# Parameter rows on another DMA queue, a weight quarter moved between transposes, and a last step ordered by token halves

## The chip, the cores and the metric

The kernel runs on one core of a Trainium2 chip. A core has five engines that run their own instruction streams and meet at semaphores: TensorE (PE in the profile; PEld is its weight load), VectorE (DVE), ScalarE (ACT), GpSimd (POOL) and SyncE (SP). Transfers run on 16 DMA engines; SyncE, ScalarE and GpSimd can each issue them through a queue of their own. The metric is the time of one execution on the device in microseconds: lower is better. Runs of the kernel before took 3287.82 to 3290.53 us, median 3289.65 us.

## The reference

One layer of a hybrid backbone over 640 tokens of width 2048: 512 latent tokens and 128 context tokens, all in float32. Cut to what the change touches:

```
sh1, sc1, g1, sh2, sc2, g2 = split(silu(c) @ w_mod + b_mod, 6)   # c for latents, c_ctx for context
h = rmsnorm(x, norm1_g) * (1 + sc1) + sh1
p = h @ w_in
...                                    # RWKV-7 time mixing and a gated MLP over p, then x + g1 * (.. @ w_out)
h = rmsnorm(x, norm2_g) * (1 + sc2) + sh2
ff = (silu(h @ w_ffn_gate) * (h @ w_ffn_up)) @ w_ffn_down
x = x + g2 * ff
y = rmsnorm(x, final_norm_g)           # the two big outputs, 512 x 2048 and 128 x 2048
```

The start computes `sc1` and `sh1` (shift and scale) and the first `h`; the end computes `... @ w_ffn_down`, the last residual sum and the final norm. The "parameter rows" are `mu_shift`, `w0`, `a0`, `k_k`, `k_a`, `r_k`, `gn_w`, `gn_b` and `norm2_g`, small vectors that the middle of the layer needs with one channel per partition.

## The kernel before

The program is written in a tile language. A planner sets each engine's order from data dependences and program order; it may move an instruction ahead of others that are not ready yet. Within the start block TensorE's order is kept as written by hand. A pool of n buffers lets n tiles of one tag be in flight; a transfer into a tile waits until the n-th tile before it has been read.

**Start (lines 212 to 348).** Tokens lie as five tiles of 128 rows. SyncE loads them (`xall`, 1 MB each), then the weights `w_mod`, in pieces `wt` of 1 MB with five buffers, and pieces of `w_in`. For each token tile the loop at line 235 squares it (ScalarE), forms `1/sqrt` on GpSimd (`rsqrt`, line 135), scales it (VectorE), and transposes it in 16 blocks on TensorE into `xnT` (line 246), copied out by VectorE and ScalarE in turn.

`quarter(g, j)` (line 297) computes 512 of the 2048 columns of scale (g = 1) or shift (g = 0): four steps, each one `wt` load and its products (line 308), a copy `ms`, four transposes and the sum into `mc`. It is a generator, and the caller decides what runs between its steps. The loop at line 333 goes over j = 0..3: `quarter(1, j)`, then `quarter(0, j)`, with products of the quarter before (`products`, three column blocks of `w_in`, lines 165 and 188) between the steps; then `h_hi` and `h_lo` for four blocks of channels. After j = 1 `rows()` issues twenty small loads on SyncE's queue (lines 265 to 278) into `rowA` and `rowB`, and after j = 2 `params()` transposes the two tiles on TensorE and copies them into `prm`.

**Middle.** Nothing in it is changed.

**End (lines 1815 to 1977).** The product with `w_ffn_down` is done for six chunks of its rows and eight pairs of column blocks n, 48 steps. Each step is one round of `seven` (line 1588): seven block products in place of eight (Strassen's scheme, in Winograd's form), in the order `PORD` = 1, 2, 3, 7, 5, 6, 4. GpSimd forms the four differences of weight blocks (`combine`); two of them, for products 6 and 4, are made in the middle of the step in the place of their sources. Every weight block is split into a rounded part `hi` (ScalarE, line 1396) and a rest `lo` (VectorE, line 1397), and a product is twelve matmuls of 320 columns, half of the tokens. In the last chunk each product's PSUM bank is first filled with the sum so far (`filled`, lines 1917 and 1918).

What follows a product is a hook, run some products later in program order (`lag`, 3 at the end). For the last chunk the hooks are those of `Last` (line 1850): they combine the seven results of step n into `cs`, two column blocks by 640 tokens, multiply by `g2` and add `x` (`out`, line 1856), and then transpose the blocks back into token rows, copy them into `acc` and add up their squares in `sse` (`rows`, line 1891). Work put into `later` runs once the next step has reached a given product: `out` for the second half of tokens after o = 2, `rows` after o = 4 (`ROWO`). For the last step, n = 0, both run after its seventh product.

When all is done, `sse` is summed over the blocks, `1/sqrt` comes from GpSimd for all five token tiles at once, and ten output tiles of 128 x 1024 (line 1968) are formed: six in one instruction on VectorE (line 1976), four by ScalarE (line 1973) and then GpSimd (line 1974). SyncE stores each.

Of the kernel before, what the change touches and what calls it, by code (L numbers as in the profile page):

```python
# [10 lines left out]
F32 = mybir.dt.float32  # L11
# [8 lines left out]
P = 128  # L20
# [37 lines left out]
FRONT = 4  # L58
REST = 6
# [28 lines left out]
def flow_step(ctx: ExitStack, tc, x_prompt, x_sample, state_rwkv, c, c_ctx, w_mod, b_mod,  # L88
# [115 lines left out]
    with ExitStack() as ph:  # L204
# [29 lines left out]
        xnT = p0.tile([P, KB, T], F32, name="xnT")  # L234
        for t in range(NT):
            xt = xall[:, t, :]
            ss = p0b.tile([P, 1], F32, name="ss")
            S.activation(junk, xt, AF.Square, accum_out=ss)
            V.tensor_scalar(ss, ss, 1.0 / D, RMS_EPS, op0=ALU.mult, op1=ALU.add)
            rs = p0b.tile([P, 1], F32, name="rs")  # L240
            rsqrt(rs, ss)
            V.tensor_scalar_mul(xt, xt, rs[:, 0:1])
            for q in range(4):
                pt = ps0.tile([P, 4, P], F32, tag="pt", name="ptx")
                for b in range(4):
                    TE.transpose(pt[:, b, :], xt[:, (4 * q + b) * P:(4 * q + b + 1) * P], ident)
                (S.copy if q % 2 else V.tensor_copy)(xnT[:, 4 * q:4 * q + 4, t * P:(t + 1) * P], pt)

# [7 lines left out]

        rowA = p0.tile([P, P], F32, name="rowA")
        rowB = p0.tile([P, P], F32, name="rowB")
        G.memset(rowB, 0.0)
        G.memset(rowA, 0.0)  # L260
        nA = C_W0

        def rows():
            for m in range(4):
                nc.sync.dma_start(rowA[C_MU + 24 * m:C_MU + 24 * m + 24, :],
                                  mu_shift[0, m, 0:3072].rearrange("(r p) -> r p", p=P))
                nc.sync.dma_start(rowA[C_MU2 + 2 * m:C_MU2 + 2 * m + 2, :],
                                  mu_shift[0, m, 3072:3328].rearrange("(r p) -> r p", p=P))
                nc.sync.dma_start(rowA[C_MU3 + m:C_MU3 + m + 1, 0:32], mu_shift[0, m:m + 1, 3328:3360])
            for off, src in ((C_W0, w0[0].rearrange("d (r p) -> (d r) p", p=P)),  # L270
                             (C_A0, a0[0].rearrange("d (r p) -> (d r) p", p=P)),
                             (C_KK, k_k[0].rearrange("(r p) -> r p", p=P)),
                             (C_KA, k_a[0].rearrange("(r p) -> r p", p=P)),
                             (C_RK, r_k[0].rearrange("(r h) n -> r (h n)", h=2)),
                             (C_GW, gn_w[0].rearrange("(r h) n -> r (h n)", h=2)),
                             (C_GB, gn_b[0].rearrange("(r h) n -> r (h n)", h=2)),
                             (C_N2, norm2_g[0].rearrange("(r p) -> r p", p=P))):
                nc.sync.dma_start(rowB[off - nA:off - nA + src.shape[0], :], src)

        def params():  # L280
            pp = ptE.tile([P, 4, P], F32, tag="ptE", name="pp")
            TE.transpose(pp[:, 0, :], rowA, ident)
            TE.transpose(pp[:, 1, :], rowB, ident)
            V.tensor_copy(prm[:, 0:nA], pp[:, 0, 0:nA])
            V.tensor_copy(prm[:, nA:C_N1], pp[:, 1, 0:C_N1 - nA])
            V.tensor_copy(prm[:, C_N2:NPRM], pp[:, 1, C_N2 - nA:NPRM - nA])

        psx.close()
        h_hi = hpool.tile([P, KB, T], F32R, tag="h_hi", name="h_hi")
        h_lo = hpool.tile([P, KB, T], F32R, tag="h_lo", name="h_lo")  # L290
        pe = pex.enter_context(tc.tile_pool(name="pe", bufs=6, space=PSUM))
        early = [[pe.tile([P, HALF], F32, tag="big", name="big") for _ in range(2)] for _ in FIRST]
# [30 lines left out]

        def products(j):
# [1012 lines left out]
    PORD = (1, 2, 3, 7, 5, 6, 4)  # L1337

# [249 lines left out]
    def seven(b11, b12, b21, b22, x, hook, nk=4, bank=fresh, last=True):  # L1588
# [6 lines left out]
        src = {1: b11, 2: b21, 3: b22, 7: t3, 5: b12, 6: b22, 4: b21}  # L1595
        order = [raw for i in PORD for raw in src[i]]

        ready = [parts(order.pop(0), nk)]
        for o, i in enumerate(PORD):
# [12 lines left out]
            if i == 3:  # L1612
# [204 lines left out]
    sse = dn.tile([P, NT, 8], F32, name="sse")  # L1817
# [32 lines left out]
    class Last:  # L1850
# [11 lines left out]
        def __call__(self, o, p):  # L1862
# [20 lines left out]
            elif o == 6:  # L1883
# [3 lines left out]
                later.append((2, lambda: (self.out(1, 1), self.out(0, 1))))  # L1887
                later.append((ROWO, self.rows))
# [15 lines left out]

    later = []
    NC = len(CHK)

    fill = [(n, i) for n in range(7, -1, -1) for i in PORD]
# [13 lines left out]
    for s, (c, n) in enumerate(steps):  # L1922
# [15 lines left out]
        for o in seven(b11, b12, b21, b22, lambda i, k: XD[i, k], None if turn else Last(n) if final else Sum(n),  # L1938
                       CHK[c], bank, not turn):
# [13 lines left out]
            if s == len(steps) - 1 and o == 5:  # L1953
                while hooks:
                    hooks.pop(0)()
# [7 lines left out]
    rs = dn.tile([P, NT], F32, name="rse")  # L1963
    V.tensor_reduce(out=rs, in_=sse, axis=AX.X, op=ALU.add)
    V.tensor_scalar(rs, rs, 1.0 / D, RMS_EPS, op0=ALU.mult, op1=ALU.add)
    rsqrt(rs, rs)
    fg = acc[:, :, 5 * HALF:5 * HALF + 256]
    for t in range(NT):
        for h in range(2):
            out = fin.tile([P, 4, 256], F32, tag=f"out{h}", name="out")  # L1970
            src, f = (ap[:, 4 * h:4 * h + 4] for ap in (acc[:, :, t * 256:(t + 1) * 256], fg))
            if t == 1 or t == 3:
                S.activation(out, src, AF.Copy, scale=rs[:, t:t + 1])
                G.tensor_tensor(out=out, in0=out, in1=f, op=ALU.mult)
            else:
                V.scalar_tensor_tensor(out=out, in0=src, scalar=rs[:, t:t + 1], in1=f, op0=ALU.mult, op1=ALU.mult)
# [31 lines left out]
```

## Time and profile before

| | |
|---|---|
| median of 3 runs | 3289.65 us (3287.82 to 3290.53) |
| the profiled execution | 3287.43 us, its span 3285.6 us |
| mean granted clock of TensorE | 0.985 |
| TensorE busy | 3141.3 us (96%) |
| VectorE busy | 2401.2 us (73%) |
| ScalarE busy | 1458.3 us (44%) |
| GpSimd busy | 1260.1 us (38%) |

The profile covers one execution. A row of a stage view (two times, then five busy times) is a stretch of the span with the busy time of each engine, the granted clock, the share of the 16 DMA engines and what they moved. A row of the timeline is start, duration, engine, line of code, instruction, output<-inputs, and in brackets how long the engine was idle before it and what ended that. A row of waits is engine and line, what it waited for, the total, the count and the longest. A queue ("SPq") holds the issues of transfers, not the transfers themselves. Matmuls are pipelined, so a busy TensorE is not one at its peak.

### The profile page before, as it was taken

The numbers are of one execution on the slowest core, as the hardware profiler recorded it, in microseconds if no ns is written. First come the engines' busy times: TensorE is split into PE (matmuls) and PEld (weight loads), VectorE is DVE, ScalarE is ACT, GpSimd is POOL, SyncE is SP. The second block draws the span as 40 slices with busy tenths as digits, with TensorE's granted clock in tenths as the row PEclk, the third lists the DMA queues.
The fourth block names the chain that finished last, engine by engine and source line by source line (L and its number), as shares of the span: only waits on it lengthen the run. The fifth ranks groups of instructions, "written<-read, shape, count | busy, mean of one in ns | idle before, by whom it ended". The sixth has DMA issues, their size and how long they took to land.

```text
span 3285.6 us, 72386 instructions
## 1 busy us (share of the span) xinstructions
PE 3141.3 (96%) x28216; PEld 2905.3 (88%) x28216; DVE 2401.2 (73%) x4152; ACT 1458.3 (44%) x3179; POOL 1260.1 (38%) x1098
## 2 busy tenths in 40 slices
PE   6899999999999999999999999999999999999996
PEld 3688888778887887889899999999999999999996
DVE  4447766776866677767877787777787777877787
ACT  3334444444444444346644444444444444444365
POOL 0001122221222113332166566566565555555543
PEclk9899999999999999999999999999999999999998
DMA  8767776767668588756434433433433454553453
GB/s 318 244 185 219 188 204 188 181 184 206 178 185 222 137 272 277 240 152 182 127 114 120 123 116 116 127 116 116 127 116 116 127 183 149 158 164 122 132 160 119
DMA packets 740142, 550.88 MB, mean 168 GB/s; under 512 B 140712, under 2 KB 673208, under 8 KB 730968
## 3 DMA queue, kind: packets, MB, share of 16 engines
q1 hardware_dynamic: 727480, 532.57, 54.3%
q0 software_dynamic: 9984, 13.13, 1.7%
q8 instruction: 222, 3.64, 0.5%
q14 instruction: 120, 0.98, 0.1%
q10 hardware_dynamic: 2336, 0.57, 0.1%
HBM read 437.79 MB, written 110.95 MB: 167 GB/s over the span
## 4 chain that ended last, share of the span: by engine, by line
PE 75%; DVE 9%; issue 6%; DMA 5%; POOL 3%; ACT 2%; SPq 0%; DVEq 0%; ACTq 0%; POOLq 0%
PE P L1611 15%; PE P L1609 15%; PE P L1610 15%; PE big L188 4%; PE big L190 4%; PE big L189 4%; PE pG L636 2%; PE pm L881 2%; DMA raw<-in_w_in_dram 2%; PE big L1455 1%; PE big L1456 1%; PE big L1457 1%; DMA wt<-in_w_mod_dram 1%; PE pblk L820 1%; DVE mx L781 1%
## 5 line engine op out<-in xcount | busy, mean ns | idle before, releaser
L1611 PE MATMUL P<-xo,lo 128*128 128x320 f32 x2352 | 728.1, 310 | 2.5 <-DVE lo L1397 2.5
L1609 PE MATMUL P<-xo,hi 128*128 128x320 f32 x2352 | 727.4, 309 | 0.7 <-ACT hi L1396 0.7
L1610 PE MATMUL P<-xo,hi 128*128 128x320 f32 x2352 | 727.4, 309 | 0.0
L1397 DVE TENSOR_TENSOR lo<-raw,hi 128x512 fp32r<-128x512 f32 x526 | 507.3, 967 | 171.4 <-ACT hi L1396 167.3
L1396 ACT CAST hi<-raw 128x512 fp32r<-128x512 f32 x526 | 327.2, 622 | 489.6 <-PE P L1610 388.7
L188 PE MATMUL big<-h_hi,hi 128*128 128x320 f32 x1376 | 450.8, 328 | 8.5 <-ACT hi L166 5.0
L1611 PEld LDWEIGHTS P<-xo,lo 128*128 128x128 f32 x2352 | 442.1, 188 | 3.8 <-DVE lo L1397 3.8
L1609 PEld LDWEIGHTS P<-xo,hi 128*128 128x128 f32 x2352 | 442.0, 188 | 1.0 <-ACT hi L1396 1.0
L1610 PEld LDWEIGHTS P<-xo,hi 128*128 128x128 f32 x2352 | 441.9, 188 | 0.0
L190 PE MATMUL big<-h_hi,lo 128*128 128x320 f32 x1376 | 435.1, 317 | 1.3 <-DVE lo L167 1.3
L189 PE MATMUL big<-h_lo,hi 128*128 128x320 f32 x1376 | 434.0, 315 | 0.7 <-DVE h_lo L345 0.7
L1525 POOL TENSOR_TENSOR raw<-raw 128x512 f32<-128x512 f32 x252 | 407.4, 1626 | 15.3 <-DVE lo L1397 3.9
L1611 PE MATMUL P<-xd,lo 128*128 128x320 f32 x1232 | 383.7, 311 | 13.8 <-DVE lo L1397 13.5
L1609 PE MATMUL P<-xd,hi 128*128 128x320 f32 x1232 | 381.8, 310 | 3.5 <-ACT hi L1396 1.7
L1610 PE MATMUL P<-xd,hi 128*128 128x320 f32 x1232 | 380.6, 309 | 0.0
L167 DVE TENSOR_TENSOR lo<-raw,hi 128x512 fp32r<-128x512 f32 x268 | 185.1, 693 | 204.7 <-ACT hi L166 198.3
L188 PEld LDWEIGHTS big<-h_hi,hi 128*128 128x128 f32 x1376 | 262.8, 191 | 74.0 <-issue 46.6
L166 ACT CAST hi<-raw 128x512 fp32r<-128x512 f32 x268 | 165.1, 618 | 250.8 <-PE big L189 124.8
L1396 ACT CAST hi<-rawd 128x512 fp32r<-128x512 f32 (+1 forms) x288 | 168.8, 587 | 242.1 <-PE P L1610 193.4
L190 PEld LDWEIGHTS big<-h_hi,lo 128*128 128x128 f32 x1376 | 263.2, 191 | 7.4 <-DVE lo L167 3.2
L189 PEld LDWEIGHTS big<-h_lo,hi 128*128 128x128 f32 x1376 | 263.3, 191 | 6.9 <-issue 3.5
L1611 PEld LDWEIGHTS P<-xd,lo 128*128 128x128 f32 x1232 | 231.2, 188 | 20.6 <-DVE lo L1397 20.2
(380 smaller groups left out, 6257.8 us busy)
## 6 DMA issues: line engine op xcount, KB each, us to landing
wt<-in_w_mod_dram SPq DMA_DIRECT2D x96, 1024.0 KB
raw<-in_w_ffn_gate_dram SPq DMA_DIRECT2D x182, 256.0 KB
raw<-in_w_ffn_up_dram SPq DMA_DIRECT2D x182, 256.0 KB
rec<-d_S SPq DMA_DIRECT2D x80, 576.0 KB
raw<-in_w_in_dram SPq DMA_DIRECT2D x172, 256.0 KB
rawd<-in_w_ffn_down_dram SPq DMA_DIRECT2D x128, 256.0 KB
raw<-in_w_out_dram SPq DMA_DIRECT2D x96, 256.0 KB
xd<-d_os SPq DMA_DIRECT2D x66, 320.0 KB
```

Of the source, the lines that this page charges most:

```text
L166: S.copy(hi, raw)
L167: V.tensor_sub(lo, raw, hi.bitcast(F32))
L188: TE.matmul(halves[hf], hi[:, k, :], h_hi[:, kb, s], start=(kb == 0), stop=False)
L189: TE.matmul(halves[hf], hi[:, k, :], h_lo[:, kb, s], start=False, stop=False)
L190: TE.matmul(halves[hf], lo[:, k, :], h_hi[:, kb, s], start=False, stop=(kb == KB - 1))
L636: TE.matmul(two[h][:, cc - c0, :], XZ[:, cc, h, :, :].rearrange("p s t -> p (s t)"), R[:, cc, :, :].rearrange("p s t -> p (s t)"), start=T ...
L1396: S.copy(hi[:, 0:nk], raw[:, 0:nk])
L1397: V.tensor_sub(lo[:, 0:nk], raw[:, 0:nk], hi[:, 0:nk].bitcast(F32))
L1525: G.tensor_tensor(out=o[:, 0:nk], in0=p[:, 0:nk], in1=q[:, 0:nk], op=ALU.subtract)
L1609: TE.matmul(ps, hi[:, k, :], xk[:, 0, :], start=f, stop=False)
L1610: TE.matmul(ps, hi[:, k, :], xk[:, 1, :], start=False, stop=False)
L1611: TE.matmul(ps, lo[:, k, :], xk[:, 0, :], start=False, stop=l)
```

## The change

At the start:

- The transposes of `rowC` (`pp`, `bmod`) and the memsets of `rowA` and `rowB` stand ahead of x's loop.
- `lead = quarter(1, 0)` is made before x's loop, and one of its steps runs after each of token tiles 2, 3 and 4 (`BEGIN` = 2). The loop over j goes on with what is left of it.
- `rows()` is called right after x's loop and issues its twenty loads on GpSimd's queue; `params()` is called after j = 1.

At the end, for the last step (n = 0) alone:

- The products are taken in the order `PEND` = 1, 6, 7, 5, 4, 3, 2. Products 6 and 4 have buffers of their own for their differences, made at the start of the step. Hooks run without lag.
- The class `End` adds each product to `cs` as it comes (`put`), in an order that completes the second half of the tokens after the fifth product, one column block of the first half after the sixth and the other after the seventh. Token tiles 3 and 4 are turned, squared and scaled (`scale`) after the fifth, tiles 0, 1 and 2 in two parts after the sixth and seventh.
- The step before it (n = 1) has its `out` and `rows` called after products 0 and 1 of the last step, not 2 and 4.

The outputs come in the order of token tiles 3, 4, 0, 1, 2. VectorE forms nine of the ten; ScalarE forms one (tile 3, second half), for which `acc` has been multiplied by `final_norm_g` in the last step (`EARLY`). GpSimd forms none.

```diff
-            for i, _ in enumerate(itertools.chain(quarter(1, j), quarter(0, j))):
+            for i, _ in enumerate(itertools.chain(lead if j == 0 else quarter(1, j), quarter(0, j))):
...
+        lead = quarter(1, 0)
         for t in range(NT):
...
                 (S.copy if q % 2 else V.tensor_copy)(xnT[:, 4 * q:4 * q + 4, t * P:(t + 1) * P], pt)
+            if t >= BEGIN:
+                next(lead)
+        rows()
...
-                nc.sync.dma_start(rowB[off - nA:off - nA + src.shape[0], :], src)
+                nc.gpsimd.dma_start(rowB[off - nA:off - nA + src.shape[0], :], src)
...
             if j == 1:
-                rows()
-            if j == 2:
                 params()
...
+    PEND = (1, 6, 7, 5, 4, 3, 2)
...
+        s6, s4 = b22, b21
+        if end:
+            s6, s4 = ([xap.tile([P, 4, P], F32, tag=next(wtags), name="rawd")] for _ in range(2))
+            combine(s6, b22, b12)
+            combine(s4, b21, s6)
...
-                later.append((2, lambda: (self.out(1, 1), self.out(0, 1))))
-                later.append((ROWO, self.rows))
+                later.append((2 if n > 1 else 0, lambda: (self.out(1, 1), self.out(0, 1))))
+                later.append((ROWO if n > 1 else 1, self.rows))
...
+    class End(Last):
+        def put(self, m, h, src, base):
+            for (lo, hi, v) in seg(h):
+                s = slice(h * HALF + lo, h * HALF + hi)
+                V.scalar_tensor_tensor(out=self.cs[m][:, s], in0=src[:, lo:hi], scalar=modc[5][:, 2 * self.n + m, v:v + 1],
+                                       in1=base[m][:, s], op0=ALU.mult, op1=ALU.add)
...
+            elif o == 4:
+                self.put(0, 1, p, cs)
+                pr = pP.tile([P, 2, 256], F32, tag="P", name="prd")
+                self.turn(pr, 0, 3, (1, 0))
+                self.turn(pr, 1, 4, (1, 0))
+                S.copy(acc[:, n, 768:1280].rearrange("p (t c) -> p t c", c=256), pr)
+                for t in range(2):
+                    self.square(pr[:, t], sse[:, 3 + t, n:n + 1])
+                scale(3, 5, 8)
+            elif o > 4:
+                m = 6 - o
+                self.put(m, 0, p, cs)
...
+    def scale(a, b, k):
+        r = rse[:, a:b]
+        V.tensor_reduce(out=r, in_=sse[:, a:b, 0:k], axis=AX.X, op=ALU.add)
+        V.tensor_scalar(r, r, 1.0 / D, RMS_EPS, op0=ALU.mult, op1=ALU.add)
+        rsqrt(r, r)
...
-    for t in range(NT):
-        for h in range(2):
+    for t in (3, 4, 0, 1, 2):
+        for h in (1, 0):
...
-            if t == 1 or t == 3:
-                S.activation(out, src, AF.Copy, scale=rs[:, t:t + 1])
-                G.tensor_tensor(out=out, in0=out, in1=f, op=ALU.mult)
+            if h and t in EARLY:
+                S.activation(out, src, AF.Copy, scale=rse[:, t:t + 1])
             else:
-                V.scalar_tensor_tensor(out=out, in0=src, scalar=rs[:, t:t + 1], in1=f, op0=ALU.mult, op1=ALU.mult)
+                V.scalar_tensor_tensor(out=out, in0=src, scalar=rse[:, t:t + 1],
+                                       in1=fg[:, 4 * h:4 * h + 4], op0=ALU.mult, op1=ALU.mult)
```

More of the change, by code (lines that the diff above doesn't have):

```diff
@@ L58 @@
 FRONT = 4
+BEGIN = 2
 REST = 6
@@ L254, in flow_step @@
         V.tensor_copy(prm[:, C_N1:C_N2], pp[:, 0, 32:48])
[L257 to L292, printed above, removed]
         mc = p0.tile([P, 2, KB, 2], F32, name="mc")
@@ new lines, in flow_step @@
+        lead = quarter(1, 0)
+        xnT = p0.tile([P, KB, T], F32, name="xnT")
+        for t in range(NT):
+            xt = xall[:, t, :]
+            ss = p0b.tile([P, 1], F32, name="ss")
+            S.activation(junk, xt, AF.Square, accum_out=ss)
+            V.tensor_scalar(ss, ss, 1.0 / D, RMS_EPS, op0=ALU.mult, op1=ALU.add)
+            rs = p0b.tile([P, 1], F32, name="rs")
+            rsqrt(rs, ss)
+            V.tensor_scalar_mul(xt, xt, rs[:, 0:1])
+            for q in range(4):
+                pt = ps0.tile([P, 4, P], F32, tag="pt", name="ptx")
+                for b in range(4):
+                    TE.transpose(pt[:, b, :], xt[:, (4 * q + b) * P:(4 * q + b + 1) * P], ident)
+                (S.copy if q % 2 else V.tensor_copy)(xnT[:, 4 * q:4 * q + 4, t * P:(t + 1) * P], pt)
+            if t >= BEGIN:
+                next(lead)
@@ L1611, in seven @@
                     TE.matmul(ps, lo[:, k, :], xk[:, 0, :], start=False, stop=l)
-            if i == 3:
+            if i == 3 and not end:
                 combine(b22, b22, b12)
@@ L1905, in flow_step @@
+    EARLY = (3,)
+    fg = acc[:, :, 5 * HALF:5 * HALF + 256]
+    def scale(a, b, k):
[3 more added lines that the diff above has]
+        rsqrt(r, r)
     later = []
     NC = len(CHK)
-    fill = [(n, i) for n in range(7, -1, -1) for i in PORD]
+    fill = [(n, i) for n in range(7, -1, -1) for i in (PORD if n else PEND)]
     banks = {}
@@ L1937, in flow_step @@
             lag[0] = LAST_LAG
-        for o in seven(b11, b12, b21, b22, lambda i, k: XD[i, k], None if turn else Last(n) if final else Sum(n),
-                       CHK[c], bank, not turn):
+        end = s == len(steps) - 1
+        work = None if turn else End(n) if end else Last(n) if final else Sum(n)
+        for o in seven(b11, b12, b21, b22, lambda i, k: XD[i, k], work, CHK[c], bank, not turn, end):
+            if end:
+                lag[0] = 0
+                while hooks:
+                    hooks.pop(0)()
             if s % 8 == 6 and c < NC - 1 and o in (2, 3, 4):
```

109 lines of the change are left out of this document (81 added, 28 removed).

## The prediction

> **What bounds the kernel now.** I read the page first, then the busy time by stage, then SyncE's own queue and its waits, then the order of time at both ends.
>
> ```profile
> span 3285.6 us, 72386 instructions
> PE 75%; DVE 9%; issue 6%; DMA 5%; POOL 3%; ACT 2%; SPq 0%; DVEq 0%; ACTq 0%; POOLq 0%
> 2.00:28.50 26.50, 12.38 (x67) 11.09 (x68) 13.35 (x27) 15.66 (x20) 2.94 (x6) 0.94 1.00 392
> 28.50:33.50 5.00, 5.00 (x49) 2.44 (x47) 1.88 (x6) 1.17 (x2) 0.00 (x0) 1.00 0.19 37
> 33.50:66.00 32.50, 23.76 (x157) 10.04 (x149) 10.34 (x26) 6.34 (x10) 0.00 (x0) 0.89 1.05 375
> 66.00:74.50 8.50, 5.56 (x36) 4.00 (x36) 3.64 (x9) 2.03 (x3) 0.00 (x0) 1.00 0.17 33
> 74.50:125.00 50.50, 41.58 (x250) 23.50 (x254) 17.15 (x41) 9.69 (x15) 0.00 (x0) 0.83 1.06 372
> 150.00:3244.00 3094.00, 3015.42 (x27441) 2821.55 (x27440) 2307.16 (x3967) 1393.71 (x3064) 1234.87 (x1070) 0.99 0.55 162
> ```
>
> The stage rows give busy time of PE, PEld, DVE, ACT and POOL, the granted clock, the DMA share and GB/s. Three regimes show. From 2 to 125 us the DMA engines are the bound (share 1.00 to 1.06, 372 to 392 GB/s), with two holes: 28.5 to 33.5 us at 0.19 and 66 to 74.5 us at 0.17. From 150 to 3244 us TensorE is busy 3015 of 3094 us; the change touches nothing there, so what the start gains or loses is passed on whole. The end is a third regime, below.
>
> What makes the two holes is read from SyncE's queue and TensorE's order:
>
> ```profile
> 6.35 11.57 SPq L304 DMA_DIRECT2D wt<-in_w_mod_dram  x5
> 31.52 6.80 SPq L304 DMA_DIRECT2D wt<-in_w_mod_dram  x6
> 57.10 1.16 SPq L265 DMA_DIRECT2D rowA<-in_mu_shift_dram  x1
> 71.90 0.32 SPq L278 DMA_DIRECT2D rowB<-in_norm_g_dram  x1
> 72.32 1.49 SPq L304 DMA_DIRECT2D wt<-in_w_mod_dram  x3
> SPq L269 <- DMA wt<-in_w_mod_dram: 3.3, 1, 3.3
> SPq L267 <- DMA wt<-in_w_mod_dram: 3.0, 2, 2.3
> 20.18 1.94 PE L246 MATMUL ptx<-ident,xall 128*128 128x128 f32 x16 [1.05 <-DVE xall L242]
> 28.21 2.09 PE L246 MATMUL ptx<-ident,xall 128*128 128x128 f32 x16 [0.39 <-DVE xall L242]
> 30.42 3.62 PE L308 MATMUL pm<-wt,cT 128*2 128x512 f32 x32
> 71.13 0.60 PE L316 MATMUL ptm<-ident,ms 128*128 128x128 f32 x4
> ```
>
> Hole 1: the five `wt` buffers are issued by 18 us; the sixth load waits until TensorE has read the first buffer, which stands behind all transposes of x (the last 16 start at 28.2, the `pm` products at 30.4). Hole 2: the twenty parameter rows hold SyncE's queue from 57.1 to 72.3 us, over 6 us of it waiting for earlier `wt` loads (rows L269, L267), and no `wt` load is issued meanwhile.
>
> The end, in order of time, then two groups with the fewest, median and most ns of one:
>
> ```profile
> 3259.18 0.31 PE L1611 MATMUL P<-xd,lo 128*128 128x320 f32 x1
> 3259.93 1.26 DVE L1859 SCALAR_TENSOR_TENSOR cd<-cd,modc,x1d 128x192 f32<-128x192 f32 x4
> 3263.83 0.20 DVE L1964 TENSOR_REDUCE rse<-sse 128x5 f32<-128x40 f32 x1 [2.63 <-ACT junk L1903]
> 3264.31 1.17 POOL L135 TENSOR_TENSOR rse<-rse,mhalf 128x5 f32<-128x5 f32 x1 [14.36 <-DVE rse L1965]
> 3265.51 15.70 DVE L1976 SCALAR_TENSOR_TENSOR out<-acc,rse 128x1024 f32<-128x1024 f32 x6 [1.29 <-POOL rse L135]
> 3266.74 12.20 POOL L1974 TENSOR_TENSOR out<-out,acc 128x1024 f32<-128x1024 f32 x4 [1.26 <-ACT out L1973]
> 3266.86 14.71 SPq L1977 DMA_DIRECT2D out_dram<-out  x10
> L1976 DVE SCALAR_TENSOR_TENSOR out<-acc,rse x6: 1273/3356/3459, 3265.5 to 3279.9; 128x1024 f32<-128x1024 f32 x6
> L1974 POOL TENSOR_TENSOR out<-out,acc x4: 2347/3317/3329, 3266.7 to 3275.6; 128x1024 f32<-128x1024 f32 x4
> ```
>
> The last product ends near 3259.2; the first output starts 6.3 us later; VectorE's outputs take 15.7 us; 4.4 us pass from their end (3281.2) to the end of the span. One VectorE output takes 1.27 us before GpSimd has begun its own and 3.36 us (median) beside it: the two engines slow each other.
>
> **The start, part by part.** Durations are of the profiled execution: 3287.43 us, its span 3285.6; the median of the runs shown, 3289.65, is 2.2 us above it, and I put the difference on that median.
>
> *Scale's first quarter between x's transposes.* No instruction is added. One step of `pm` products (a quarter of the 3.62 us, 0.9 us) follows the transposes of each of x's tiles 2, 3 and 4. Tile 2's end at 22.1, so the first buffer comes free near 23 instead of 31.5, the next two near 28 and 31: loads are in the queue before the fifth drains at 28.5. VectorE and ScalarE have time for their part (13.35 and 15.66 of 26.5 us). Hole 1 is worth 5.0 x (1.05 - 0.19) / 1.05 = 4.1 us. Bounds: 0 (something else holds the transposes back, below) to 5.0. I take 4.1.
>
> *Parameter rows on GpSimd's queue.* SyncE loses twenty issues and `wt` loads follow each other. Hole 2 is worth 8.5 x (1.05 - 0.17) / 1.05 = 7.1 us. What GpSimd then pays, by the nearest rows:
>
> ```profile
> L672 POOL DMA_DIRECT2D dd<-GB x128: 537/537/786, 231.4 to 1040.9; - x128
> L800 POOL DMA_DIRECT2D TB<-d x64: 662/664/1012, 315.0 to 1088.4; - x64
> DMA to landing us min/median/max: 2.5/4.3/8.1
> L135 POOL TENSOR_TENSOR rs<-ss,mhalf x5: 548/548/571, 10.2 to 26.2; 128x1 f32<-128x1 f32 x5
> 10.76 0.21 POOL L260 MEMSET rowA<- 128x128 f32 x1
> ```
>
> Twenty issues by 0.54 to 0.66 us are 11 to 13 us on an engine with 2.94 busy us there (at the worst issue, 1.01 us, 20 us). If they stand behind the fifth `rs` (ends 26.8), they end by 40 (worst 47) and the last lands by 55. `params` moves one round earlier, behind the transposes now at 71.1, some 67 us with hole 1 gone; TensorE's order is written out by hand, so everything behind `params` would wait if rows were late. Slack is 12 us or more: cost 0, covered by the other loads of that round. The planner can also hoist them: `rowA`'s memset, written behind all five `rs`, ran at 10.76 ahead of four of them. Then `rs` waits up to 11 us, x's transposes with it, and hole 1 stays; hole 2 closes all the same. I take 7.1, bounds 4 to 8.5.
>
> Here a rule speaks against the change. The Trainium skill (SBUF — State Buffer, "SBUF: two separate sides") says that GpSimd cannot write the descriptors of its DMAs while VectorE runs an instruction that takes both ports, and states 3.1 us in place of 0.62 for such an overlapped transfer. By that, twenty would take an estimated 62 us, `params` would wait for them until about 93 us, and the change would end some 7 us slower in all. The trace agrees only with the page's undisturbed figure: L672 and L800 never exceed 1.01 us, with VectorE 75% busy from 150 us on. That is the slower rival below.
>
> The remaining moves at the start (`pp`, `bmod`, the memsets) keep their count and lie beside loads: 0.
>
> **The end, part by part.** *The last step.* It keeps its seven products; its order becomes 1, 6, 7, 5, 4, 3, 2.
>
> ```profile
> 3244.00:3259.50 15.50, 15.30 (x108) 15.00 (x107) 11.73 (x21) 9.59 (x27) 3.24 (x2) 1.00 0.18 52
> 3246.47 1.72 DVE L1859 SCALAR_TENSOR_TENSOR cd<-cd,modc,x1d 128x192 f32<-128x192 f32 x2
> 3248.71 1.71 DVE L1859 SCALAR_TENSOR_TENSOR cd<-cd,modc,x1d 128x192 f32<-128x192 f32 x2
> L1859 DVE SCALAR_TENSOR_TENSOR cd<-cd,modc,x1d 128x320 f32<-128x320 f32 x4 | 2.2, 546 | 3.3 <-DMA x1d<-d_x 3.3
> L1880 DVE TENSOR_TENSOR tp<-P,tp 128x320 f32<-128x320 f32 x2 | 1.0, 491 | 0.1
> L1903 ACT ACTIVATE junk<-prd 128x256 f32<-128x256 f32 x15 | 6.1, 408 | 0.1
> L1903 ACT ACTIVATION_READ_ACCUMULATOR junk<-prd 128x1 f32 x15 | 3.3, 223 | 0.0
> ```
>
> GpSimd's two differences in this stage (3.24 us) are replaced by two made ahead, in buffers of their own; it is idle most of the step before, so 0. VectorE: before the last product the output sums take two adds by 0.49, four scaled additions by 0.55 and eight by 0.32 (1.26 / 4), 5.7 us, where six adds and two scaled additions take 4.0 now; `EARLY`, 1024 columns, adds 1.3; the two pairs at 1.71 that GpSimd slowed fall to 0.63 each, 2.1 less. That is 11.73 + 1.7 + 1.3 - 2.1 = 12.6 of 15.5 us. ScalarE gets five squares more, by 0.41 + 0.22, 12.7. TensorE stays the bound, but with no lag a product's sums stand before the next split. I add 1.0 us of stalls (bounds 0 and 3.2, all of GpSimd's time given back) and 0.4 for transposes that move ahead of the last product.
>
> *From the last product to the first late output.* Now 6.3 us. Afterwards: one scaled addition 0.55, three transposes 0.5, three squares of 128 columns, each at most 0.41 + 0.22 (1.4 to 1.9, I take 1.4), the reduction and its scaling 0.4, the power of three elements between its 0.55 and 1.17, 0.87, handovers 0.5: 4.2 us. Gain 2.1 (bounds 1.0 and 3.0).
>
> *Outputs.* Ten stay. Token tiles 3 and 4 are ready about when the last product ends; one goes to ScalarE and three to VectorE, into its idle time during the squares; three by 1.27 overfill it, so I charge 0.7. Six are left: 6 x 1.27 = 7.6 us with no GpSimd beside them, against 15.7: gain 8.1 (lower bound 0, if the pace were set by something other than GpSimd; but the 1.27 row is the same instruction on the same data). The DMAs: ten of 0.52 MB at 392 GB/s are 13.4 us, hardly less than the time they now have, so I charge 0.5 for queueing; the last 4.4 us stay.
>
> The sum of the end: -8.1 - 2.1 + 0.4 + 1.0 + 0.7 + 0.5 = -7.6 us. Of the whole: -4.1 - 7.1 - 7.6 = -18.8, that is 3289.65 - 18.8 = 3270.9 us, some 0.57% faster.
>
> **The rivals.** *A, only the end pays:* the row issues are hoisted ahead of `rs`, hole 1 stays and the freed time of hole 2 is half lost to the late x; for it speaks the hoisted memset, against it that SyncE kept the rows in program order. -3.6 - 7.6: 3278.5. *B, only the start pays:* with no lag the last step stalls at each product and the early outputs stand in front of the last sums; the step loses 3.2, the outputs' gain halves: -11.2 - 1.4: 3277. Against it stand 2.9 free us of VectorE. *C, no change:* both A and B, or the middle replanned by some us: -3.6 - 1.4, 3285. *D, slower:* one mechanism, GpSimd's row issues held by VectorE, so that `params` waits. It decides where the rows land later than 67 + 18.8 = 86 us, at 2.95 us an issue. The farthest row is a GpSimd instruction beside VectorE, 3.32 (L1974): 27 + 20 x 3.32 + 8 = 101 us, 34 us of waiting less 18.8: 3305. Against it: 1.01 us was the worst of 192 issues.
>
> **How the numbers follow.** Forecast 0.60, A 0.13, B 0.13, C 0.07, D 0.07. A change under 0.2% (6.6 us) can't be told from none here. Faster is the first three, 0.86; same C, 0.07; slower D, 0.07. The range runs from 3265, with the start's upper bounds (5.0 + 8.5) and an end of -11.1 (no stall, no queueing, early outputs not in the way, 3.0 for the chain), to 3284, where the end pays nothing and the start half; it leaves out C and D.
>
> **What would show it.** Right: no stretch under half DMA share between 20 and 110 us; the sixth `wt` load near 23 us; the last one landing some 11 us sooner; rows issued on GpSimd in about 0.55 us each and landed before `params`; VectorE's outputs at 1.27 us with six of them behind the last `rse`; last product to end of span 17 us instead of 26. Wrong: `rs` late at the start, a TensorE gap ahead of `params`, `lo` waits in the last step, or outputs that stay above 2 us with GpSimd idle.

## The result, and the profile after

The changed kernel takes 3273.93 us (median of 4 runs, 3272.34 to 3275.93) where the kernel before took 3290.09 us beside it (4 runs, 3287.82 to 3290.58): a ratio of 0.995, interval 0.9936 to 0.9963, or 12 to 21 us. The forecast was 3270.9 us, 18.8 us less than before.

That is too coarse to judge the prediction's terms. Its terms are stage times, so I read each stage from the traces. First the start, by the busy time by stage of the changed kernel. The columns are the stretch and its length, the busy time of PE, PEld, DVE, ACT and POOL with their instructions, the granted clock, the DMA share and GB/s.

```profile
2.00:28.50 26.50, 11.85 (x68) 9.85 (x69) 11.15 (x27) 14.38 (x18) 16.63 (x25) 1.00 1.00 384
28.50:33.50 5.00, 5.00 (x48) 2.78 (x46) 3.77 (x5) 2.35 (x4) 0.16 (x1) 1.00 1.04 363
33.50:66.00 32.50, 25.41 (x176) 13.08 (x168) 11.01 (x26) 6.43 (x10) 0.00 (x0) 0.95 1.05 378
66.00:74.50 8.50, 6.01 (x46) 2.92 (x42) 6.34 (x17) 3.62 (x6) 0.00 (x0) 1.00 1.06 372
74.50:112.00 37.50, 32.80 (x219) 21.39 (x220) 13.60 (x32) 8.01 (x13) 0.00 (x0) 0.95 1.06 374
```

Both holes are closed: 1.04 where 0.19 stood, 1.06 where 0.17 stood. The DMA engines are now the bound without a break from 2 to 112 us, and TensorE still waits there for `wt`, 8.9 us in seven waits, where it was 15.4 us in nine.

What this is worth is read from one instruction at the end of each stage. Here are, in order of time, the `wt` issues, a ScalarE cast just behind the start and a GpSimd difference just ahead of the last two steps, first of the changed kernel, then the same two instructions of the kernel before.

```profile
6.99 30.77 SPq L253 DMA_DIRECT2D wt<-in_w_mod_dram  x11
136.31 0.62 ACT L550 CAST wh<-wl 128x512 fp32r<-128x512 f32 x1
3204.01 1.30 POOL L1530 TENSOR_TENSOR t<-rawd 128x512 f32<-128x512 f32 x1 [7.80 <-DMA rawd<-in_w_ffn_down_dram]
```

```profile
147.76 0.62 ACT L546 CAST wh<-wl 128x512 fp32r<-128x512 f32 x1
3212.16 1.55 POOL L1525 TENSOR_TENSOR t<-rawd 128x512 f32<-128x512 f32 x1 [7.90 <-DVE tp L1880]
```

Eleven `wt` loads follow each other from 7 to 38 us where five and six stood apart. The cast comes 147.76 - 136.31 = 11.45 us sooner. But 3.06 ms later the difference comes only 3212.16 - 3204.01 = 8.15 us sooner: in this pair of executions 3.3 us were lost on the way, in code that the change does not touch.

The end of the changed kernel, in order of time:

```profile
3253.37 1.28 DVE L2060 SCALAR_TENSOR_TENSOR out<-acc,rse 128x1024 f32<-128x1024 f32 x1 [0.82 <-POOL rse L136]
3253.59 0.31 PE L1622 MATMUL P<-xd,lo 128*128 128x320 f32 x1
3254.55 11.86 SPq L2062 DMA_DIRECT2D out_dram<-out  x10
3254.57 0.55 DVE L1924 SCALAR_TENSOR_TENSOR cd<-P,modc,cd 128x320 f32<-128x320 f32 x1
3255.27 0.69 PE L1977 MATMUL prd<-ident,cd 128*128 128x128 f32 x3 [1.37 <-ACT junk L1981]
3257.43 0.18 DVE L1989 TENSOR_REDUCE rse<-sse 128x3 f32<-128x27 f32 x1
3257.88 0.86 POOL L136 TENSOR_TENSOR rse<-rse,mhalf 128x3 f32<-128x3 f32 x1 [4.55 <-DVE rse L1990]
3258.78 7.27 DVE L2060 SCALAR_TENSOR_TENSOR out<-acc,rse 128x1024 f32<-128x1024 f32 x6 [0.97 <-POOL rse L136]
```

Six outputs run without a break in 7.27 us behind the last power (L136), where VectorE took 15.7 us before. From the last product's start to the end of the span it is 16.9 us, where it was 26.4. One cost shows too: VectorE's early output, started 0.2 us ahead of the last product, holds the last scaled addition (L1924) back to 3254.57.

The stage times of every profiled execution, in one table. "Start" is how much sooner (minus) or later the work behind the start runs than in the kernel before: the median over all instructions that ran there at 155 to 200 us, each against its counterpart. "Middle" is what that median changes by until 3205 us, and "end" what it changes by from there to the end of the span. The last column is the time in the middle in which TensorE's granted clock was half of full. (The cast above gives -11.45 for the -11.5 of the first row, and the GpSimd difference 3.3 for the 3.4.)

| kernel | start | middle | end | half clock, us |
|---|---|---|---|---|
| the change | -11.5 | +3.4 | -7.1 | 47.8 |
| the change again | -10.1 | +4.5 | -7.4 | 41.0 |
| before again | -1.2 | +5.7 | -0.8 | 41.0 |
| before | 0 | 0 | 0 | 44.4 |
| start only | -10.2 | +8.8 | -0.2 | 54.6 |
| end only | -0.6 | -9.3 | -7.3 | 27.3 |
| quarter only | -5.2 | +2.8 | -0.4 | 47.8 |
| rows only | -4.1 | +7.7 | -0.5 | 51.2 |
| differences on VectorE | -10.6 | +1.4 | -6.6 | 44.4 |
| two outputs on GpSimd | -10.1 | +11.8 | -5.5 | 64.9 |
| rows late | -11.5 | +11.9 | -7.1 | 54.6 |
| late differences | -10.4 | +5.5 | -9.4 | 44.4 |

Start and end repeat within 1.5 us for equal code. The middle, equal code in all twelve, spreads over 21 us.

### The profile page after: what moved, and what is told of

It is laid out like the page before. It is cut to its first block, busy times and chain, and to the rows that moved or that the text cites. A ratio compares the mean times of both kernels' runs of the same rounds, so it can differ in the third digit from the quotient of the medians.

```text
span 3270.5 us, 72414 instructions
## 1 busy us (share of the span) xinstructions
PE 3135.4 (96%) x28216; PEld 2904.2 (89%) x28216; DVE 2409.8 (74%) x4160; ACT 1454.6 (44%) x3181; POOL 1267.4 (39%) x1115
## 4 chain that ended last, share of the span: by engine, by line
PE 71%; DVE 11%; issue 6%; DMA 5%; POOL 3%; ACT 2%; SPq 0%; DVEq 0%; POOLq 0%; ACTq 0%
PE P L1622 15%; PE P L1620 15%; PE P L1621 15%; PE big L189 4%; PE big L191 3%; PE big L190 3%; PE pG L640 2%; PE pm L885 2%; DVE mx L785 1%; DMA raw<-in_w_in_dram 1%; DMA wt<-in_w_mod_dram 1%; PE big L1460 1%; PE big L1462 1%; PE big L1461 1%; PE big L1017 1%
## 5 line engine op out<-in xcount | busy, mean ns | idle before, releaser
L1402 DVE TENSOR_TENSOR lo<-raw,hi 128x512 fp32r<-128x512 f32 x526 | 517.6, 988 | 158.7 <-ACT hi L1401 154.1
L168 DVE TENSOR_TENSOR lo<-raw,hi 128x512 fp32r<-128x512 f32 x268 | 185.7, 695 | 200.2 <-ACT hi L167 194.0
```

The source lines that it names most:

```text
L168: V.tensor_sub(lo, raw, hi.bitcast(F32))
L1402: V.tensor_sub(lo[:, 0:nk], raw[:, 0:nk], hi[:, 0:nk].bitcast(F32))
```

## The experiments

**The start alone and the end alone.** One kernel has the diff's part up to the moved `params` only, one has the rest only.

```
start_only: rows on nc.gpsimd, lead = quarter(1, 0) between the transposes; the end as before
end_only:   PEND, End, scale, outputs by VectorE; the start as before
```

> Only the start of the change (quarter between x's transposes, rows on GpSimd's queue, params one round earlier); the end as before. Theory: the two DMA holes are closed, the first instructions behind the start come 11 to 12 us sooner (11.5 in the changed kernel), and what the middle then gives back (3.5 us in the changed kernel's profile) is no part of the change but depends on when TensorE's granted clock drops to half: 3290 - 11.4 = 3278.7 us, with 3 us either way. Rival: the middle gives 3.5 us back in each execution: 3282. Second rival, that the start's gain is lost altogether: 3290.

> Only the end of the change; the start as before. Theory: the end gains 7.2 us by itself (the changed kernel's distance to the one before grows by that from step 46 to the end), and the middle keeps its length, since its start does not move: 3282.9 us. Rival (B of the prediction): only the outputs gain, the last step gives most of it back: 3287 to 3289.

Start only: 3279.89 us, ratio 0.9974 (0.9962 to 0.9986), 4.6 to 12.5 us less. End only: 3281.99 us, ratio 0.9978 (0.9964 to 0.9992), 2.6 to 11.8 us less. Each is of use alone, so rivals A, B and C are out. The stage times agree: the start alone gives 10.2 us at the start and nothing at the end, the end alone 0.6 and 7.3. By the ratios they are worth 8.6 and 7.2 us, 15.8 together, beside 16.5 for both.

**The start's two parts, each alone.**

```
lead_only: lead = quarter(1, 0), next(lead) between the transposes; rows() on nc.sync, as before
rows_only: rows() on nc.gpsimd, params() one round earlier; no next(lead) between the transposes
```

> Only scale's first quarter between x's transposes; the rows stay on SyncE's queue and params after j = 2, the end as before. Theory: hole 1 (28.5 to 33.5 us) is closed, hole 2 stays and comes 4 us sooner: 3290 - 4.1 = 3286 us. Rival: the loads of hole 1 are hidden anyway, the wait moves to hole 2: 3290.

> Only the parameter rows on GpSimd's queue with params after j = 1; the quarter stays behind x's transposes, the end as before. Theory: hole 2 is closed, hole 1 stays; the rows' issues between the five rs hold x's transposes back by 2 us (30.3 to 32.2 in the changed kernel), and that makes hole 1 longer here: 3290 - 7.1 + 2 = 3285 us. Rival: x's transposes set nothing, 3283.

Quarter only: 3284.6 us, ratio 0.9989 (0.9979 to 1.0). Rows only: 3289.48 us, ratio 1.0 (0.9991 to 1.001). At the start they gain 5.2 and 4.1 us, 9.3 together, where the seven profiles with the whole start gain 10.1 to 11.5. The rows alone had been expected to gain about 5. The busy time by stage says why the second is not the larger one. The quarter alone:

```profile
28.50:33.50 5.00, 4.28 (x40) 1.85 (x38) 2.30 (x6) 1.76 (x3) 0.00 (x0) 1.00 1.05 386
33.50:66.00 32.50, 24.78 (x171) 12.76 (x164) 10.26 (x24) 6.44 (x10) 0.00 (x0) 0.95 0.92 328
66.00:74.50 8.50, 2.69 (x19) 1.25 (x17) 6.71 (x15) 2.87 (x4) 0.00 (x0) 0.80 0.67 237
```

The rows alone:

```profile
28.50:33.50 5.00, 4.50 (x34) 3.64 (x35) 3.58 (x6) 2.10 (x4) 0.56 (x1) 0.71 0.23 79
33.50:66.00 32.50, 24.89 (x160) 9.93 (x153) 10.22 (x25) 5.96 (x10) 0.00 (x0) 0.84 0.99 353
```

With the quarter alone, hole 1 is closed (1.05), and hole 2 stands elsewhere with its old size: (1.05 - 0.92) x 32.5 / 1.05 + (1.05 - 0.67) x 8.5 / 1.05 = 4.0 + 3.1 = 7.1 us. With the rows alone, hole 1 stays (0.23, 3.9 us) and reaches into the next stretch (0.99 in place of 1.05, 1.9 us): it has grown, because the row issues hold x's transposes back, and the `pm` products behind them start at 33.05 us where they started at 30.42. What hole 2's closing gives is partly lost there, while hole 1 is open. The rows-only median, unchanged within 3 us, does not show the 4.1 us at the start; in the one profile taken the middle was 7.7 us longer, and the median leaves open whether that is chance.

**Where the rows stand on GpSimd.** The row issues of the changed kernel, in order of time, with the VectorE instructions beside them:

```profile
11.47 1.41 POOL L294 DMA_DIRECT2D rowB<-in_w_dram  x1
11.49 1.28 DVE L305 TENSOR_SCALAR xall<-xall,rs 128x2048 f32<-128x2048 f32 x1 [0.46 <-POOL rs L136]
12.88 0.56 POOL L281 DMA_DIRECT2D rowA<-in_mu_shift_dram  x1
15.99 0.59 POOL L136 TENSOR_TENSOR rs<-ss,mhalf 128x1 f32<-128x1 f32 x1
16.53 1.47 POOL L281 DMA_DIRECT2D rowA<-in_mu_shift_dram  x1
16.61 1.29 DVE L305 TENSOR_SCALAR xall<-xall,rs 128x2048 f32<-128x2048 f32 x1 [1.88 <-POOL rs L136]
24.79 1.04 PE L257 MATMUL pm<-wt,cT 128*2 128x512 f32 x8
28.10 0.56 POOL L136 TENSOR_TENSOR rs<-ss,mhalf 128x1 f32<-128x1 f32 x1 [0.72 <-DVE ss L302]
30.27 1.97 PE L309 MATMUL ptx<-ident,xall 128*128 128x128 f32 x16
```

The planner hoisted them between the `rs`, which is rival A's mechanism: VectorE waits 1.88 us for an `rs` that stands behind row issues. And four of the twenty issues take 1.41 to 1.57 us in place of 0.50 to 0.56: each began as VectorE began to scale a tile of x, and ended 0.1 us after it (11.49 + 1.28 = 12.77, the issue at 12.88). To price both, I let the rows stand behind all `rs`, by zeroing their tiles from x's last scaled tile:

```
-        G.memset(rowB, 0.0)
-        G.memset(rowA, 0.0)
...
+        for r in (rowB, rowA):
+            G.tensor_tensor(out=r, in0=xall[:, 4, 0:P], in1=xall[:, 4, 0:P], op=ALU.subtract)
         rows()
```

> The changed kernel with one edit: rowB and rowA are zeroed by subtracting a scaled piece of x's last token tile from itself, not by a memset, so that none of the twenty row issues can stand ahead of any rs on GpSimd. Theory (from 2 to 112 us the DMA engines are the bound, so neither the hoisted issues nor x's transposes 2 us later cost anything): twenty issues between 28 and 40 us, x's transposes end near 30.3 instead of 32.2, both holes stay closed, and the work behind the start comes 11.2 to 12 us sooner than before, as with the change as it is. Rival A (hoisting costs): it comes 13 to 14 us sooner. Rival D (issues held by VectorE): issues of 1.4 us and more beside VectorE's long instructions, rows landing behind 65 us, params waits, and it comes less than 9 us sooner.

3280.82 us (one run); the start gains 11.5 us, as in the changed kernel. In order of time:

```profile
25.67 0.55 POOL L136 TENSOR_TENSOR rs<-ss,mhalf 128x1 f32<-128x1 f32 x1 [1.81 <-DVE ss L302]
28.16 1.97 PE L309 MATMUL ptx<-ident,xall 128*128 128x128 f32 x16
28.34 0.77 POOL L294 DMA_DIRECT2D rowB<-in_w_dram  x1
29.11 0.56 POOL L281 DMA_DIRECT2D rowA<-in_mu_shift_dram  x1
41.38 0.52 POOL L294 DMA_DIRECT2D rowB<-in_norm_g_dram  x1
```

x's last transposes start 2.1 us sooner (28.16 for 30.27), one issue of twenty is above 0.56 us (0.77), the last ends at 41.9, and the start gains what the changed kernel's profile shows. So neither the hoisting nor the four held issues costs more than the 1.5 us by which starts of equal code differ: the start is bound by the DMA engines, and 2 us of TensorE lie in cover.

**Equal code again.** The changed kernel and the kernel before once more, with no edit.

> The changed kernel once more, nothing edited. Theory: the length of the middle (150 us to step 46) is set in each execution by how long TensorE's granted clock is at half, 44 us in the kernel before, 48 in the changed one and 27 to 55 in the four part kernels, at some 0.6 us of time for each; so a second profile of the same program shows another length of the middle, by several us, with the same 11.4 us gained by 150 us and the same 7.2 gained at the end, and the median over many runs comes to -18.6 against the kernel before: 3269.6 if that stays at 3288.2. Rival: the middle's 3.5 us belong to the changed program: the same length again, and 3273.

> The kernel before once more, nothing edited, for its profile alone. Theory: its middle differs from that of the first profile by several us, and by about 0.6 us for each us that the granted clock is longer or shorter at half; the start to 150 us and the end from step 46 stay within 0.6 us. Rival: the two profiles agree in the middle within 1 us.

The change again: 3274.56 us, ratio 0.9956 (0.9938 to 0.9974), not the 3269.6 expected, and its middle is much like the first (4.5 for 3.4 us), as the rival of that expectation had it. This pair alone would put the 3.4 us down to the change. Before again, one run: 3291.19 us; its start and end lie 1.2 and 0.8 us from the first, more than the 0.6 expected. The pair of the kernel before is the test of "the middle passes it on whole". In its second execution the two instructions named above stand at

```profile
146.53 0.62 ACT L546 CAST wh<-wl 128x512 fp32r<-128x512 f32 x1
3216.14 1.30 POOL L1525 TENSOR_TENSOR t<-rawd 128x512 f32<-128x512 f32 x1 [7.36 <-DVE cd L1879]
```

that is 1.23 us sooner, and then 3.98 us later: the same program lost 5.2 us between them. So one profile can't tell whether the 3.4 us belong to the change. Part of the cause is TensorE's granted clock. The same 15 us of the span, first of the changed kernel, then of its repetition:

```profile
1295.00:1310.00 15.00, 13.05 (x192) 10.94 (x192) 10.59 (x34) 5.57 (x27) 10.29 (x14) 0.66 0.69 210
```

```profile
1295.00:1310.00 15.00, 13.23 (x243) 10.67 (x245) 12.34 (x40) 7.20 (x36) 9.72 (x13) 1.00 0.80 251
```

At a mean clock of 0.66, 192 matmuls against 243, with TensorE busy about equally long. Over the twelve rows of the table the middle grows by 0.55 us for each us at half clock (correlation 0.88, and 0.77 without the row "end only"). Half speed would cost an estimated 0.5 us where TensorE is the bound. Single rows lie up to 4.4 us off that line, and no run sets the clock, so this is a correlation.

What comes ahead of a stretch of half clock can be counted in the traces. The clock changes in steps of 3.41 us. In the middle of all twelve profiles there are 78 steps at full clock in which TensorE was busy for less than half of the time, and 73 of them were followed by half clock; of 94 steps busy for 50 to 60%, 15 were; of 10133 busy for more than 75%, 8. A pause of TensorE can fall into one step or be split between two. The step from 1294.9 us of the changed kernel was busy 54%, and half clock followed; the two steps there of its repetition were busy 62 and 86%, and none followed. So executions of one program can differ by where its pauses fall in the steps. What causes the rest of the scatter stays open.

**The step before the last.** The stage table of the end, in us. A step runs from the start of its first matmul to the start of the next step's first; the last step, to the start of its last matmul ("last product").

| | step before last | last step | last product to last power's end | from there to the end |
|---|---|---|---|---|
| before | 15.90 | 14.87 | 6.30 | 20.14 |
| before again | 15.53 | 14.87 | 6.30 | 20.15 |
| the change | 17.62 | 15.50 | 5.15 | 11.73 |
| the change again | 17.69 | 15.49 | 5.15 | 11.74 |
| differences on VectorE | 18.25 | 15.51 | 5.15 | 11.74 |
| late differences | 15.68 | 15.52 | 5.14 | 11.73 |
| two outputs on GpSimd | 17.45 | 15.51 | 5.15 | 13.82 |

The step before the last, whose own products do not change, is some 2 us longer (1.7 to 2.2 us in the change). In the trace of the changed kernel, GpSimd's differences and TensorE's waits in it:

```profile
3220.12 1.56 POOL L1530 TENSOR_TENSOR t<-rawd 128x512 f32<-128x512 f32 x1 [8.16 <-DVE tp L1892]
3221.75 8.09 POOL L1530 TENSOR_TENSOR rawd<-rawd 128x512 f32<-128x512 f32 x5
3228.75 0.41 PE L1622 MATMUL P<-xd,lo 128*128 128x320 f32 x1 [0.89 <-DVE lo L1402]
3231.38 0.41 PE L1622 MATMUL P<-xd,lo 128*128 128x320 f32 x1 [0.46 <-DVE lo L1402]
```

Five differences in a row: the last step's two new ones (`s6`, `s4`) stand ahead of this step's own two, which come 2 us later than before. But TensorE does not wait for a difference. It waits for `lo`, VectorE's rests of weight blocks. Here is VectorE ahead of the first of these waits, in the changed kernel and then in the kernel before:

```profile
3224.05 1.37 DVE L1402 TENSOR_TENSOR lo<-rawd,hi 128x512 fp32r<-128x512 f32 x1
3225.35 2.75 DVE L1871 SCALAR_TENSOR_TENSOR cd<-cd,modc,x1d 128x192 f32<-128x192 f32 x2
3228.02 0.68 DVE L1402 TENSOR_TENSOR lo<-t,hi 128x512 fp32r<-128x512 f32 x1
```

```profile
3231.99 0.68 DVE L1397 TENSOR_TENSOR lo<-rawd,hi 128x512 fp32r<-128x512 f32 x1
3232.59 1.71 DVE L1859 SCALAR_TENSOR_TENSOR cd<-cd,modc,x1d 128x192 f32<-128x192 f32 x2
3234.22 0.68 DVE L1397 TENSOR_TENSOR lo<-t,hi 128x512 fp32r<-128x512 f32 x1
```

The same three instructions: 1.37 for 0.68 and 2.75 for 1.71 us beside GpSimd's run, so that the third starts 3.97 us behind the first where it was 2.23. These 1.7 us are what the step grew by (15.90 to 17.62). Two experiments. The first makes the two new differences on VectorE:

```
-            combine(s6, b22, b12)
-            combine(s4, b21, s6)
+            for o_, p_, q_ in ((s6, b22, b12), (s4, b21, s6)):
+                V.tensor_sub(o_[0][:, 0:nk], p_[0][:, 0:nk], q_[0][:, 0:nk])
```

> The changed kernel with the two differences that the last step newly makes ahead (for products 6 and 4) on VectorE, not GpSimd. In the changed kernel GpSimd makes four differences in a row (6.58 us) in step 46, VectorE's sums beside it take 2.75 us in place of 1.71, and TensorE waits 0.89 and 0.46 us for lo; step 46 lost 1.7 us. Theory (GpSimd beside VectorE costs that): step 46 gets 1 to 1.7 us back, less up to 0.6 for VectorE's two differences of 0.68: the end 0.5 to 1.5 us shorter. Rival (VectorE is simply full there): no gain or a loss of 1 us.

3274.12 us, ratio 0.9962 (0.9948 to 0.9975); the step takes 18.25 us, where a gain of 0.5 to 1.5 us was expected. Now the two differences stand ahead of the splits on VectorE itself, and TensorE waits 2.88 us for one `lo`, 0.66 before. The second leaves them on GpSimd, in buffers of the step before the last that come free late, so that they must follow its own two:

```
-            s6, s4 = ([xap.tile([P, 4, P], F32, tag=next(wtags), name="rawd")] for _ in range(2))
+            s6, s4 = [[xap.tile([P, 4, P], F32, tag=t, name="rawd")] for t in [next(wtags) for _ in range(6)][:3:-1]]
```

> The changed kernel with one edit: the last step's two differences s6 and s4 are made in buffers that come free later (those of the step before's second half), so on GpSimd they stand behind the step before's own two differences instead of ahead of them. Theory (GpSimd's five differences in a row hold up the step before): that step takes 15.5 to 15.9 us again instead of 17.6, the last step stays at 15.5, and the end is some 2.0 us shorter than the changed kernel's; of the median, which moves by 8 us from run to run, perhaps 2 us, about 3272 us. Rival (the step is held by VectorE's load of splits and scaled additions, not by GpSimd's order): the step before stays at 17.4 to 17.7 us. Second rival (the two differences are now late for the last step): the last step grows from 15.5 to 17 us or more and nothing is won.

3271.85 us, ratio 0.994 (0.992 to 0.996). GpSimd in order of time:

```profile
3222.57 1.30 POOL L1530 TENSOR_TENSOR t<-rawd 128x512 f32<-128x512 f32 x1 [7.70 <-DMA rawd<-in_w_ffn_down_dram]
3223.95 1.43 POOL L1530 TENSOR_TENSOR rawd<-rawd 128x512 f32<-128x512 f32 x1
3227.41 3.31 POOL L1530 TENSOR_TENSOR rawd<-rawd 128x512 f32<-128x512 f32 x2 [2.03 <-DVE lo L1402]
3232.28 3.04 POOL L1530 TENSOR_TENSOR rawd<-rawd 128x512 f32<-128x512 f32 x2 [1.56 <-DVE lo L1402]
```

The step's own pair comes first, 4.8 us after the first difference, and the new pair follows. The step takes 15.68 us and the last step still 15.52: the end is 9.4 us shorter than before's, against 7.1 and 7.4 for the change. Here the new pair runs in a place where VectorE is idle for 1.43 us, and no `lo` holds TensorE longer than 0.34 us. The place of the two differences in GpSimd's order was the cause; the differences are the same. This version is the fastest by stage times; its median lies 2.1 us under the change's, less than the spread of single runs (3265.11 to 3277.55) can tell.

**Two outputs back on GpSimd.** Token tile 1's outputs go to ScalarE and GpSimd again, the rest as changed:

```
+            elif t == 1:
+                S.activation(out, src, AF.Copy, scale=rse[:, t:t + 1])
+                G.tensor_tensor(out=out, in0=out, in1=fg[:, 4 * h:4 * h + 4], op=ALU.mult)
```

> The changed kernel with token tile 1's two outputs made by ScalarE and then GpSimd, as before the change; the other seven stay on VectorE. Theory (the two engines hold each other up): the two GpSimd instructions take 3.3 us each and so do the VectorE outputs beside them, two or three of four; from the last rse to the end of the span 2 to 4 us more than in the changed kernel, though VectorE has two outputs less. Rival (the output stage is bound by the stores): no change, within 0.5 us.

3274.74 us, ratio 0.9968 (0.9955 to 0.9982). In order of time:

```profile
3263.75 13.71 SPq L2065 DMA_DIRECT2D out_dram<-out  x10
3267.97 9.13 DVE L2063 SCALAR_TENSOR_TENSOR out<-acc,rse 128x1024 f32<-128x1024 f32 x4 [0.97 <-POOL rse L136]
3269.20 5.62 POOL L2061 TENSOR_TENSOR out<-out,acc 128x1024 f32<-128x1024 f32 x2 [1.26 <-ACT out L2060]
```

Four outputs of VectorE take 9.13 us beside two of GpSimd, where six take 7.27 alone. From the last power to the end it is 13.82 us in place of 11.73. Fewer outputs for VectorE, and 2.1 us more.

## Why the prediction was right, and where not

**The total** came out: 18.8 us forecast, 16.2 measured by the medians (12 to 21). By stages the seven profiles with the whole start gain 10.1 to 11.5 us there, and the two of the change 7.1 and 7.4 at the end.

**The start, 11.2 us: right as a sum, wrong in its parts.** Hole 1 closed and hole 2 closed, and the bound behind them was DMA. But 4.1 and 7.1 are not what the two edits are worth alone, 5.2 and 4.1 in one profile each; the 1.1 more of the first is within what starts of equal code differ by, the 3.0 less of the second is not. The working added two holes as if independent, while the row issues lengthen hole 1 when it is open. It did name this (x's transposes wait on hoisted issues) but only as a reason that hole 1 might stay. It did not see that the issues lengthen hole 1, or that the other edit covers that.

**Rival A's hoisting came, and cost nothing.** The order was as that rival had it, with four `rs` 1.2 to 2.4 us later than where the rows stand behind them. Its price was wrong: hole 1 closed all the same, because the `pm` step behind tile 2, at 24.8 us where I had put it near 23, still frees its buffer ahead of 28.5.

**Rival D came in kind, not in size.** "L672 and L800 never exceed 1.01 us" was no bound for these issues: four were held to 1.41 to 1.57 us. The condition was the instruction beside them, not VectorE's being busy: held beside a scaling of 128x2048 in SBUF, not beside the work of the middle. By the Trainium skill's rule (SBUF — State Buffer, "SBUF: two separate sides") the descriptors wait until such an instruction of VectorE ends, and here the trace agrees: the end of each of the four lies 0.1 us behind it. The rule's sum in the prediction, by 3.1 us for each of twenty, fails since four of twenty met such an instruction, and for 0.9 us more each. And 1.57 us, the longest, lies well under the 2.95 us an issue from which that rival decides, or 2.55 if the 8 us of landing that its other sum counts are counted here too.

**"What the start gains or loses is passed on whole"** can't be upheld as a statement on one execution. The middle varies by up to 21 us between executions with equal code in it, more than the start's gain. Over many runs it is not settled either: by their ratios the eight kernels that have all or part of the new start gain 0.1 to 5.1 us less than their starts and ends do (the start alone 8.6 where they give 10.4). About 1 us of that may be the profile they are compared with, since the second execution of the kernel before comes 1.2 and 0.8 us sooner there; that the middle takes some of the start's gain back is not excluded. "A change under 0.2% can't be told" was too narrow for single runs: those of the kernel before reach from 3278.07 to 3294.14 us in one set of 34. What a change of that size does is read from its stage's own time.

**The end, 7.6 us; 7.1 to 7.4 measured.** Term by term, in the changed kernel's profile:

- Outputs: forecast -8.1, with 0.5 for the queueing of the stores, -7.6; measured 20.14 to 11.73, -8.4. Six at 1.28 us, where 1.27 was forecast, and the last 4.4 us stayed (3266.05 to 3270.47). The charge for queueing was not needed: the ten stores leave within 11.86 us.
- From the last product to the last power: forecast -2.1, with 0.7 for early outputs in the way, -1.4; measured 6.30 to 5.15, -1.15. The charge for the early output is right in place and size: it holds the last scaled addition back 0.6 us.
- The last step: forecast +0.4 for moved transposes and +1.0 for stalls; measured 14.87 to 15.50, +0.6. There were no stalls: TensorE is idle for 0.02 us of the 15.50, 0.20 of the 14.87. The growth is the transposes'.
- The step that failed is "it is idle most of the step before, so 0". GpSimd had the time, but not at that place: the two differences made ahead run beside VectorE's splits and scaled additions, which take up to twice as long there, and TensorE waits for the splits. The prediction knew that the two engines slow each other and counted it for the outputs and the last step, not here. Measured +1.7 to +2.2 (15.90 and 15.53 to 17.62 and 17.69), and taken away by the order alone (15.68).

The end's sum came out by luck: the outputs and the last step were each 0.8 us better than charged, which nearly made up for this one. (The forecast's best end, -11.1, leaves out the 0.4 for transposes; with it the range would start 0.4 us higher.)

## What to carry to other kernels

Idle time of an engine covers added work only if the work stands behind what is due sooner and beside an engine that has slack: check the order in its queue and what runs next to it, not its busy share, and where a planner sets the order, give the early work a buffer that comes free late. Two gaps in a stage bound by transfers need not be additive; price each with the other one open and closed. When a long stage with equal code varies by more than the change is worth, judge the change by the times of its own stages, and compare two executions of the same program before anything is said about the rest.

## What was not expected of the hardware

- In the changed kernel's start, DMA issues on GpSimd take 0.50 to 0.56 us, but 1.41 to 1.57 us when they begin beside VectorE's scaling of 128x2048 float elements, ending 0.1 us after it. With the rows late, one beside VectorE's copies of 128x512 out of `ptx` took 0.77 us.
- TensorE's granted clock falls to half for stretches of 3.4 to 13.7 us in the middle, where it is busy over 97% of the time: 27 to 65 us in all in each of twelve profiles, with 0.55 us of time for each. Some places recur (one at 582 to 595 us in every profile), others differ between executions of the same program. The Trainium skill (TensorE: Matmul & The Clock Gate, "Part 1: The HAM clock gate (the "warmup" mystery)") has windows of 3.4 us, after an idle one of which the clock is halved; the lengths here are multiples of 3.4 us too, but the step ahead need not be idle: with TensorE busy for up to half of it, 73 of 78 were followed by half clock.
- VectorE's output of 128x1024 takes 1.28 us alone and up to 3.46 us beside GpSimd's product of the same shape, which takes 2.35 to 3.33. That was the largest term of the change, 8.4 us.
